# Right-side SBUF tiles moved down by 992 bytes, to whole KBs

## The chip, the cores and the metric

The kernel runs on one core of a Trainium2 chip. The metric is the time of the device for one execution, in microseconds (us), as the median over several runs. Three runs of the kernel before gave 1609.98, 1612.35 and 1612.64 us.

## What is computed

Two layers of a diffusion transformer on 512 latent tokens and 256 context tokens with 1024 features, all in float32. Cut to what matters:

```
for i in range(2):
    mod = split(silu(c) @ ada_w[i] + ada_b[i], 6)          # one set for latents, one for context
    h   = rmsnorm(x, norm_mix_g[i]) * (1 + mod[1]) + mod[0]
    x  += mod[2] * (recurrence(h) if i == 0 else latent_attention(h))
    h   = rmsnorm(x, norm_ffn_g[i]) * (1 + mod[4]) + mod[3]
    g, u = split(h @ ffn_w_in[i], 2)                       # 1024 -> 2 x 2816
    x  += mod[5] * ((silu(g) * u) @ ffn_w_out[i])          # 2816 -> 1024
return rmsnorm(x_latent, final_norm_g)
```

In layer 0 context tokens are carried along everywhere. In layer 1 they only feed keys and values, so the feed-forward part of layer 1 has 512 tokens.

## The kernel before

Features lie on the 128 partitions, tokens along the free dimension: the latents are columns 0 to 511 of a row of 768, the context columns 512 to 767. Every large product is made in three passes. A weight tile and an activation tile are each kept as two float32r parts (h for high, l for low) whose sum is the float32 value, and `mm3` (line 671) issues wh x xh, wh x xl and wl x xh for each feature tile. The weights (128x128) are loaded into TensorE, the activations move through it, and each matmul has a weight load of its own.

The activations that move are of two kinds. The normed and modulated activations, hh and hl, are written by `norm_tile` (line 553: VectorE makes nt, ScalarE hh, VectorE hl) and read by the input products of the recurrence (p, g, u), of the attention latents (ckv, kr, cq) and of the feed-forward part (f, f00g and so on). All others are made inside a stage: ah and al (the gated hidden features, read by the products fo), uh and ul (read by the gates ga), mh and ml (read by lo), cqh and cql (read by q), oh and ol (read by wo), kh and kl (read by the scores s).

In layer 0 most products go over both groups of tokens, so a 512-column matmul and a 256-column matmul alternate (48 matmuls a product with 8 feature tiles). In layer 1 the input products of the feed-forward part and cq take the 512 latent tokens alone. So do two entry phases, in `entry` (line 611), where the products of the second group of tokens follow its norm.

Weights come through `Stream` (line 62): the SP queue loads them whole, ScalarE copies the high part (line 103), VectorE or GpSimd makes the low part (line 115). The modulation vectors come from ada_w: tiles "ada" of 128x1024 are loaded by GpSimd's queue (line 212). In layer 0 they move through TensorE (line 480), in layer 1 VectorE sums them up (lines 430 to 440).

The order of the work on each engine is written out by hand (the strings START, ATTENTION and STEPS); from `manual_schedule` (line 172) on nothing reorders it. Two stacks share each partition's memory. Pools from the left grow up, and pools with side="right" grow down from the end at 229344 bytes, which is 223 KB and 992 bytes. The right side holds, in turn:

```
tile             from line   begins at (bytes)   over a whole KB   bytes
hh0              154         180192              992               24576
hl0              155         204768              992               24576
ada (2 buffers)  211         172000, 176096      992               4096 each
wh, wl of "more" 1335        221152, 225248      992               4096 each
hh1, hl1         1345        188384, 204768      992               16384 each
```

Every tile on the left that a product of line 675 reads begins at a whole KB: ah at 103 KB, al at 127 KB, cqh at 119 KB, kh at 177 KB (and 180 KB), the weights wh and wl from 37 KB to 69 KB. A feature tile's row is 3072 bytes in hh0, hl0, ah and al, and 2048 in hh1 and hl1. The weights of the first unit of layer 1's feed-forward part come from "more"; all other weights lie on the left.

Of the kernel before, what the change touches and what calls it, by code (L numbers as in the profile page):

```python
# [9 lines left out]
F32 = mybir.dt.float32  # L10
# [25 lines left out]
ENTRY_AT = (12, 6)   # products of the first group that follow the statistics, and the spread  # L36
# The first norm and its first products in the order of their parts, see the layer
# [5 lines left out]
# Latent attention in the order of its parts: a letter and its arguments, see mla_mix  # L43
# [18 lines left out]
class Stream:  # L62
    """Weights in the order in which TensorE takes them: loaded whole, split into two float32r
    parts whose sum is the float32 value."""
# [45 lines left out]
    def _low(self, i):  # L110
        """Second part of a unit: what the first leaves of the float32 value."""
        load, n, pieces = self.units[i]
        raw, (hi, lo) = self.raw[load], self.tiles[i]
        for dst, src in pieces:
            self.low_engine.tensor_tensor(dst(lo), src(raw), dst(hi).bitcast(F32), op=ALU.subtract)  # L115
        self.loads[load][2] -= 1
        if self.loads[load][2] == 0:
            del self.raw[load]
            self.fill()
# [20 lines left out]
def kernel(ctx, tc, x, c, ctx_in, c_ctx, ada_w, ada_b, norm_mix_g, norm_ffn_g, ffn_w_in,  # L140
# [11 lines left out]
    hstack, adastack = ExitStack(), ExitStack()  # L152
    hpool = hstack.enter_context(tc.tile_pool(name="h0", bufs=1, side="right"))
# [34 lines left out]
    # shift and scale of the first norm, in parts of the features: first tile, tiles  # L188
# [47 lines left out]
    def std_units(w, col0, ncols, row0=0, kt=KT, ucols=P):  # L236
        """Columns [col0, col0 + ncols) of w as one load, in units of ucols columns."""
        ln = st.load(kt * ncols, lambda t: nc.sync.dma_start(
            t[:, :kt * ncols].rearrange("p (k n) -> p k n", k=kt),
            w[row0:row0 + kt * P, col0:col0 + ncols].rearrange("(k p) n -> p k n", p=P)))  # L240
        ids = []
        for u in range(ncols // ucols):
            dst = lambda t: t[:, :kt * ucols].rearrange("p (k n) -> p k n", k=kt)
            src = lambda t, u=u: t[:, :kt * ncols].rearrange("p (k n) -> p k n", k=kt)[
                :, :, u * ucols:(u + 1) * ucols]
            ids.append(st.unit(ln, kt * ucols, [(dst, src)]))
        return ids
# [14 lines left out]
    # The recurrence in the order of its parts. n = block of 256 features, k = feature tile in it, d = direction:  # L262
    # u n k = input tile, c n k = its convolution, g n k = gate branch tile, G n k = its gelu,
    # t T n d k = gates, w = next weights, e n d k = decay and gated input, q n d k = scale of the input, s n d k = states,
    # m n = gated states of a block, o n m = tile of the output product, a = part of a modulation vector
# [105 lines left out]
    gcol = lambda w: cols_b[:, 96 + w * 8:96 + w * 8 + 8]  # mix0 mix1 ffn0 ffn1  # L371
# [6 lines left out]
    def ada0_step(q, kq):  # L378
        """Products of a part of the first two chunks: groups of columns j = (chunk, tile)."""
        if kq == 0:  # L380
            ada_ps["q"] = psa.tile([P, 512], F32, name=f"psada0{q}", tag="ada")
        ps = ada_ps["q"]
        t = ada0_tiles.pop((q, kq))
        w = PARTS0[q][1]
        for k2 in range(QK):
            k = kq * QK + k2
            for j in range(2 * w):
                c0 = j % w * P
                pe.matmul(ps[32 * j:32 * j + 32, :P], csil[:, k, :], t[:, k2, j // w, c0:c0 + P],
                          start=k == 0, stop=k == KT - 1)  # L390
# [15 lines left out]
    def ada_evac(wait=False):  # L406
        """Columns of a finished chunk; a step after its products, so that TensorE does not wait."""
        if ada_state["evac"] is None:
            return
        i, l, ch, sb = ada_state["evac"]  # L410
        if wait and ada_state["calls"] < 2:
            ada_state["calls"] += 1
            return
        ada_state["evac"] = None
        px = ps_aux(f"adax{i}")
        for cc in range(2):
            pe.transpose(px[:, cc * P:(cc + 1) * P], sb[:, cc * P:(cc + 1) * P], ident)
        pv = px[:, :256].rearrange("p (c j r) -> p j c r", c=2, j=4)
        for v in range(2):
            dve.tensor_tensor(mod[:, l, ch, v, :].rearrange("p (j c) -> p j c", j=4), pv[:, :, :, v],  # L420
                              adab(l, ch).rearrange("p (j c) -> p j c", j=4), op=ALU.add)
        if ch in (1, 4):
            w = l + (2 if ch == 4 else 0)
            for v in range(2):
                dve.scalar_tensor_tensor(gm[:, w, v, :], mod[:, l, ch, v, :], 1.0, gcol(w),
                                         op0=ALU.add, op1=ALU.mult)

    def ada_sum(i, t, ch, k):
        """One feature tile of a chunk of layer 1 on VectorE; a later product with ones adds up the partitions."""
# [95 lines left out]
    def rstd(ss, dst, n):  # L525
        """dst = (ss / n + eps) ** -0.5, tokens on partitions."""
        dve.tensor_scalar(dst, ss, 1.0 / n, EPS, op0=ALU.mult, op1=ALU.add)
        act.activation(dst, dst, AF.Sqrt)
        dve.reciprocal(dst, dst)

    def col_rstd(sqs, s, n, name):
        """rst of the tokens of s, from the partial sums of squares in the tiles sqs."""
# [8 lines left out]
    def diagonals(s, name):  # L541
        """rst of the tokens of s on diagonals; bcast spreads them."""
        dg = tmp.tile([P, T], F32, name=f"dg_{name}", tag="nt")
        for i, t in enumerate(tiles_of(s)):
            dve.tensor_scalar(dg[:, i * P:(i + 1) * P], ident, rst[:, t:t + 1], None, op0=ALU.mult)
        return dg

    def bcast(s, dg, R):
        """R[p, token] = rst of the tokens of s, on all partitions."""
# [3 lines left out]
    def norm_tile(k, w, l, ch, R, roff, group, hh, hl):  # L553
        """Modulated norm of feature tile k, tokens of the group, into hh; returns what makes hl."""
# [10 lines left out]
    class Norm:  # L565
        """Norm and modulation of one group of tokens, in pieces that stand between other work."""
# [23 lines left out]
    def boundary(last_group, na, after=lambda i: None, at=(1, 3, 2)):  # L590
        """The last products of a stage for the second group of tokens, and the norm of the first."""
# [19 lines left out]
    def entry(units, na, nb, nk=2, at=ENTRY_AT):  # L611
        """First products of a stage: the first group of tokens while the norm of the second is made.
        units: (unit, PSUM tile, offset, with the first group)."""
# [39 lines left out]
    def residual(m, ps, l, ch, group, stat):  # L653
        """x tile m += gate * product; the sum of squares on the way where a norm comes next."""
# [16 lines left out]
    def mm3(ps, wh, wl, xh, xl, parts, first, last, off=0):  # L671
        """ps += w^T x in three passes of the split parts."""
# [18 lines left out]
    Rs = acc  # L691

    # recurrence constants
# [10 lines left out]
    def lru_constants():  # L704
        """softplus(-lambda) by its series of atanh, in three pieces; the gates' biases."""
# [27 lines left out]
    # The norm of the first layer and the products that take its tiles as they come  # L733
# [56 lines left out]
    def lru_out(n, m, mt, group, stat=False):  # L790
        """Two feature tiles of the state times w_out, tile m of the result."""
# [12 lines left out]
    def gate(n, d, kk, g, uh, ul):  # L804
        """Gate product g of direction d, feature tile kk of block n."""
# [13 lines left out]
    def decay(n, d, kk, y):  # L819
        """Decay a, the square of the input's scale and the gated input."""  # L820
# [15 lines left out]
    def states(n, d, kk):  # L836
        """Input term and the state sequence."""
# [193 lines left out]
    def mla_mix():  # L1031
# [42 lines left out]
        def rope(dst, src, sh, scale):  # L1074
            """dst = scale * rotated src."""
# [18 lines left out]
        # latents: statistics, norms, the rotated key  # L1094
# [58 lines left out]
        # keys, values and queries of the heads: products (small letters) and their float32r parts  # L1153
# [33 lines left out]
        def uses(u, n):  # L1187
            """The n-th use of a unit is its last."""
# [20 lines left out]
        # rotated queries of two heads: their float32r parts on the two halves of the partitions, so that  # L1209
        # one pass of 128 rows carries two of the three products  # L1210
# [21 lines left out]
        # scores and softmax of 128 queries, transposes, products with the values for 256  # L1232
# [120 lines left out]
    class Final:  # L1353
        """Last norm of one group of tokens, back to tokens on partitions."""
# [23 lines left out]
        def last(self):  # L1378
            """The same with the last feature tile's squares apart, on both engines, in halves."""
# [29 lines left out]
def _rope_tables():  # L1409
    """cos and signed sin of the two axial positions, features on rows, tokens on columns."""  # L1410
# [32 lines left out]
```

## Time and profile before

| | us |
|---|---|
| runs, median of 3 | 1612.35 |
| runs, lowest and highest | 1609.98, 1612.64 |
| profiled execution, span from first to last instruction | 1610.0 |
| profiled execution, its own time | 1610.0 (the page gives the span; the lowest run is 1609.98) |
| TensorE busy in the span | 1556.2 |
| VectorE, ScalarE, GpSimd busy | 807.4, 603.7, 254.1 |

A matmul's listed duration overlaps with that of the next one: matmuls are pipelined. What a matmul costs in a steady stream is therefore the step from its start to the next start, which the chain of waits gives as time over count. [...]

### The profile page before, as it was taken

What the parts mean: (1) busy time and instruction counts of PE and PEld (TensorE: products, weight loads), DVE (VectorE), ACT (ScalarE), POOL (GpSimd) and SP (SyncE); (2) the same over time, 40 slices, a digit from 0 to 9 for tenths busy, and PEclk for the clock granted to TensorE, in tenths of its full rate; (3) what the DMA queues carried; (4) which work ended last, traced back from release to release, by engine and by line L of the source; (5) the groups of instructions that cost most, each with busy time, mean ns of one, the idle gap of its engine ahead of it and who ended that gap; (6) DMA issues with size and microseconds to landing.
All of it is one profiled execution on the core that took longest, in us unless ns stands there. A gap on an engine that the chain in (4) does not pass through costs nothing.

```text
span 1610.0 us, 20936 instructions
## 1 busy us (share of the span) xinstructions
PE 1556.2 (97%) x8895; PEld 1320.6 (82%) x8895; DVE 807.4 (50%) x1068; ACT 603.7 (37%) x812; POOL 254.1 (16%) x212
## 2 busy tenths in 40 slices
PE   7999988979999999999999999999998999999998
PEld 5887877868888888888888877888888888888887
DVE  5666768686545433443322466655536343233234
ACT  5486564733221111221122233666644232232223
POOL 3233332350000000000000323111125000000002
PEclk8999999999999999999999999999999999999999
DMA  9333343220344333344311222110011223223222
GB/s 358 117 108 129 105 131 105 97 87 26 107 137 139 116 121 114 115 141 138 103 55 40 66 60 69 29 42 27 27 66 66 79 89 121 79 82 127 79 66 92
DMA packets 121406, 155.09 MB, mean 96 GB/s; under 512 B 5212, under 2 KB 104145, under 8 KB 121313
## 3 DMA queue, kind: packets, MB, share of 16 engines
q1 hardware_dynamic: 109456, 112.21, 21.2%
q0 software_dynamic: 11552, 41.02, 7.8%
q8 instruction: 70, 1.15, 0.3%
q10 hardware_dynamic: 304, 0.53, 0.1%
q14 instruction: 24, 0.19, 0.0%
HBM read 151.64 MB, written 2.10 MB: 95 GB/s over the span
## 4 chain that ended last, share of the span: by engine, by line
PE 84%; DVE 11%; ACT 3%; issue 1%; DMA 0%; SPq 0%; DVEq 0%; ACTq 0%
PE fo L675 18%; PE f L675 14%; PE s L1242 4%; PE lo L675 3%; PE ga L675 3%; PE wo L675 2%; PE o L1284 2%; PE p L675 2%; PE g L675 2%; PE t L1260 1%; DVE yc L782 1%; DVE tg L845 1%; DVE hl L561 1%; PE u L675 1%; PE q L675 1%
## 5 line engine op out<-in xcount | busy, mean ns | idle before, releaser
L103 ACT ACTIVATE wh<-raw 128x1024 fp32r<-128x1024 f32 (+2 forms) x195 | 191.3, 1011 | 195.1 <-PE fo L675 154.9
L115 POOL TENSOR_TENSOR wl<-raw,wh 128x1024 fp32r<-128x1024 f32 (+3 forms) x66 | 155.5, 2367 | 337.9 <-ACT wh L103 296.6
L675 PE MATMUL fo<-ah,wl 128*128 128x512 f32 (+1 forms) x552 | 167.5, 348 | 0.0
L675 PE MATMUL fo<-ah,wh 128*128 128x512 f32 (+1 forms) x552 | 167.5, 348 | 0.0
L675 PE MATMUL fo<-al,wh 128*128 128x512 f32 (+1 forms) x552 | 167.0, 347 | 0.0
L115 DVE TENSOR_TENSOR wl<-raw,wh 128x1024 fp32r<-128x1024 f32 (+1 forms) x129 | 151.1, 1199 | 2.7 <-ACT wh L103 2.6
L675 PE MATMUL f<-hl,wh 128*128 128x512 f32 x336 | 130.7, 393 | 0.0
L675 PE MATMUL f<-hh,wl 128*128 128x512 f32 x336 | 130.7, 393 | 0.0
L675 PE MATMUL f<-hh,wh 128*128 128x512 f32 x336 | 130.7, 393 | 0.0
L669 POOL TENSOR_TENSOR acc<-acc,sq 128x256 f32<-128x256 f32 (+1 forms) x52 | 51.6, 994 | 494.9 <-ACT sq L667 487.6
L656 DVE SCALAR_TENSOR_TENSOR xT<-fo,mod,xT 128x512 f32<-128x512 f32 (+1 forms) x76 | 46.6, 636 | 155.5 <-PE fo L675 155.2
L212 POOL DMA_DIRECT2D ada<-in_ada_w_dram x78 | 41.9, 538 | 511.5 <-DVE ada L440 384.6
L995 ACT ACTIVATE ah<-sg 128x768 fp32r<-128x768 f32 (+1 forms) x44 | 32.5, 739 | 196.0 <-DVE sg L994 196.0
L675 PEld LDWEIGHTS fo<-ah,wh 128*128 128x128 f32 x552 | 93.5, 189 | 14.7 <-ACT wh L103 0.4
L675 PEld LDWEIGHTS fo<-ah,wl 128*128 128x128 f32 x552 | 93.4, 189 | 13.6
L675 PEld LDWEIGHTS fo<-al,wh 128*128 128x128 f32 x552 | 93.2, 188 | 13.5
L994 DVE TENSOR_TENSOR sg<-sg,f 128x512 f32<-128x512 f32 (+1 forms) x21 | 14.7, 700 | 144.1 <-ACT sg L993 141.1
L675 PEld LDWEIGHTS f<-hh,wh 128*128 128x128 f32 x336 | 62.6, 188 | 15.0
L675 PEld LDWEIGHTS f<-hh,wl 128*128 128x128 f32 x336 | 62.6, 188 | 14.9
L675 PEld LDWEIGHTS f<-hl,wh 128*128 128x128 f32 x336 | 62.6, 188 | 14.9
L993 ACT ACTIVATE sg<-f 128x512 f32<-128x512 f32 x20 | 12.0, 598 | 155.0 <-PE f L675 155.0
L440 DVE SCALAR_TENSOR_TENSOR ada<-ada,csil,ada 128x1024 f32<-128x1024 f32 x42 | 53.9, 1282 | 32.1 <-DMA ada<-in_ada_w_dram 31.6
(656 smaller groups left out, 3480.9 us busy)
## 6 DMA issues: line engine op xcount, KB each, us to landing
raw<-in_ffn_w_in_dram SPq DMA_DIRECT2D x44, 1024.0 KB, 4.9
ada<-in_ada_w_dram POOLq DMA_DIRECT2D x78, 512.0 KB, 4.1
raw<-in_ffn_w_out_dram SPq DMA_DIRECT2D x16, 1024.0 KB, 4.9
ada<-in_ada_w_dram SPq DMA_DIRECT2D x32, 256.0 KB, 5.5
raw<-in_ffn_w_out_dram SPq DMA_DIRECT2D x8, 768.0 KB, 4.6
raw<-in_lru_w_in_dram SPq DMA_DIRECT2D x10, 512.0 KB, 5.0
raw<-in_lru_gate_w_dram SPq DMA_DIRECT2D x16, 256.0 KB, 3.0
raw<-in_lru_w_out_dram SPq DMA_DIRECT2D x8, 512.0 KB, 4.0
```

What stands on the lines that cost most here:

```text
L103: nc.scalar.activation(dst(hi), src(raw), AF.Copy)
L115: self.low_engine.tensor_tensor(dst(lo), src(raw), dst(hi).bitcast(F32), op=ALU.subtract)
L212: eng.dma_start(t, ada_w[l, k * P:(k + 1) * P, ch * D:(ch + 1) * D])
L440: dve.scalar_tensor_tensor(t, t, csil[:, k, 0:1], ada_ps["lat"], op0=ALU.mult, op1=ALU.add)
L561: return lambda: dve.scalar_tensor_tensor(hl[:, k, s], t[:, :n], mod[:, l, ch, v, k:k + 1], hh[:, k, s].bitcast(F32), op0=ALU.add, op1=ALU ...
L656: dve.scalar_tensor_tensor(xT[:, m, s], ps[:, s], mod[:, l, ch, v, m:m + 1], xT[:, m, s], op0=ALU.mult, op1=ALU.add)
L669: accs.append(lambda: nc.gpsimd.tensor_tensor(acc[:, s], acc[:, s], sq[:, s], op=ALU.add))
L675: pe.matmul(ps[:, off + s.start:off + s.stop], a, b[:, s], start=first and i == 0, stop=last and i == 2)
L782: dve.scalar_tensor_tensor(y[:, s0:s1], ps[:, s0 + o:s1 + o], convw(tap, k), y[:, s0:s1], op0=ALU.mult, op1=ALU.add)
L995: act.activation(ah[:, j, :n], sg[:, :n], AF.Copy)
L1242: pe.matmul(ps[:, o:o + 384], x, y[:, k0:k1], start=j == 0, stop=j == 4)
L1284: pe.matmul(ps[:, :256], x[:, t % 4, hs], y[:, t, :], start=t == 0 and j == 0, stop=t == NT - 1 and j == 2)
```

## The change

A pool "skip" is opened on the right side before all others, with one tile of 248 float32 values in each partition (992 bytes), which GpSimd fills with zeros once and which nothing reads. All later tiles of the right side thus begin 992 bytes lower: hh0 at 179200 bytes (175 KB), hl0 at 203776 (199 KB), hh1 at 187392 (183 KB), hl1 at 203776 (199 KB), the ada tiles at 171008 and 175104 (167 and 171 KB), the weights of "more" at 220160 and 224256 (215 and 219 KB). The left side stays where it is. The rest of the diff takes out comments and doc strings.

```diff
     tmp = ctx.enter_context(tc.tile_pool(name="tmp", bufs=2))
     hstack, adastack = ExitStack(), ExitStack()
+
+    skip = ctx.enter_context(tc.tile_pool(name="skip", bufs=1, side="right")).tile([P, 248], F32, name="skip")
+    nc.gpsimd.memset(skip, 0.0)
     hpool = hstack.enter_context(tc.tile_pool(name="h0", bufs=1, side="right"))
     hh = hpool.tile([P, KT, T], F32R, name="hh0")
     hl = hpool.tile([P, KT, T], F32R, name="hl0")
```

## Rows read from the trace of the kernel before

**Rows 1.** The page: span, busy time of each engine, and the chain's shares by engine.
```profile
span 1610.0 us, 20936 instructions
...
PE 1556.2 (97%) x8895; PEld 1320.6 (82%) x8895; DVE 807.4 (50%) x1068; ACT 603.7 (37%) x812; POOL 254.1 (16%) x212
...
PE 84%; DVE 11%; ACT 3%; issue 1%; DMA 0%; SPq 0%; DVEq 0%; ACTq 0%
```

**Rows 2.** Windows, layer 1: PE, PEld, DVE, ACT, POOL busy us (count), clock, DMA share, GB/s.
```profile
1254.00:1321.00 67.00, 67.00 (x289) 53.94 (x288) 22.18 (x24) 18.78 (x24) 0.00 (x0) 1.00 0.29 95
1321.00:1365.00 44.00, 44.00 (x196) 36.40 (x195) 16.98 (x19) 11.79 (x13) 0.00 (x0) 1.00 0.35 114
```

**Rows 3.** Chain of waits, 512-column streams of layer 1: start, us, engine, product, line, matmuls.
```profile
967.19 4.90 PE cq L675 x21
...
1188.10 5.50 PE wo L675 x24
...
1248.57 5.60 PE f11g L675 x24
1254.17 67.20 PE f L675 x288
1321.37 43.55 PE fo L675 x192
1364.91 89.60 PE f L675 x384
1454.51 43.55 PE fo L675 x192
1498.06 67.20 PE f L675 x288
```

**Rows 4.** Chain of waits inside the entry phases of layer 0 and layer 1.
```profile
380.58 0.70 PE f01g L675 x3
```
```profile
956.70 1.40 PE ckv L675 x6
```

**Rows 5.** Chain of waits, layer 0, products with 512 and 256 columns in turn.
```profile
411.74 8.48 PE f002u L675 x48
...
506.44 25.44 PE fo L675 x144
...
618.24 8.32 PE f012u L675 x48
...
711.76 24.98 PE fo L675 x144
```

**Rows 6.** Timeline of TensorE, scores of layer 1 (384 columns, two a row).
```profile
1048.99 0.51 PE L1242 MATMUL s<-kl,qh 128*128 128x384 f32 x2
1049.34 0.51 PE L1242 MATMUL s<-kh,ql 128*128 128x384 f32 x2
```

**Rows 7.** Timeline of TensorE, modulation products: 128 columns from the left, 256 from ada.
```profile
24.94 1.52 PE L389 MATMUL psada<-ada,csil 128*32 128x128 f32 x48
```
```profile
108.10 1.07 PE L480 MATMUL psada<-ada,csil 128*32 128x256 f32 x16
```

**Rows 8.** Groups by line and form: line, engine, operation, shapes, count | busy us, mean ns.
```profile
L561 DVE SCALAR_TENSOR_TENSOR hl<-nt,mod,hh 128x512 fp32r<-128x512 f32 x24 | 18.0, 749 | 3.6 <-ACT hh L560 3.0
L782 DVE SCALAR_TENSOR_TENSOR yc<-u,cols_d,yc 128x511 f32<-128x511 f32 x12 | 9.0, 746 | 3.7 <-ACT yc L778 3.4
...
L558 DVE SCALAR_TENSOR_TENSOR nt<-xT,gm,R_m1b 128x512 f32<-128x512 f32 x8 | 5.9, 748 | 4.1 <-PE R_m1b L551 3.9
```

**Rows 9.** Timeline of all engines at the start.
```profile
0.74 0.20 POOL masks.py:197 MEMSET ident<- 128x128 f32 x1 [0.29 <-POOLq L1429]
...
2.08 0.31 POOL masks.py:199 TENSOR_SCALAR_AFFINE_SELECT ident<-ident 128x128 f32<-128x128 f32 x1
...
4.55 7.03 PE L506 MATMUL xtr<-ident,xtok 128*128 128x128 f32 x40 [1.10 <-DMA xtok<-in_ctx_dram]
...
22.18 0.48 PE L513 MATMUL pt<-ident,rows_b 128*128 128x128 f32 x1
```

## The prediction, written before the run

> **What bounds the kernel now.** I read the page first: TensorE is busy for 97% of the 1610.0 us span and the chain of work that ended last is 84% TensorE [rows 1]. An edit that leaves every instruction where it is can gain only if it shortens a step of that chain. [...]
>
> Then I read the chain as steps, time over count. The products f, f11g and cq, which move hh and hl, take 67.20 / 288 = 89.60 / 384 = 5.60 / 24 = 4.90 / 21 = 233.3 ns a matmul. The products fo, which move ah and al, take 43.55 / 192 = 226.8 ns [rows 3]. Both have 512 columns, fresh weights for each matmul, the same clock, and no gap. [...] The difference, **6.5 ns a matmul**, is the whole matter.
>
> What separates the kinds? Not the pitch of a row: cq moves hh0 (3072 bytes a row) and f moves hh1 (2048), and both step at 233.3, while ah has 3072. [...]
>
> **The change, part by part.**
>
> *Streams of 512 columns on hh and hl.* In layer 1's feed-forward part they are 24 + 288 + 384 + 288 = 984 matmuls, all in the chain [rows 3]. Cq adds 3 tiles x 8 x 3 = 72, the latent group of ckv and kr another 72, and the latent group of layer 0's entry 72. In the entry phases the step is the same, 0.70 us for three and 1.40 for six [rows 4]; per feature tile the nine matmuls take 2.1 us against 2 x 0.75 = 1.5 us of VectorE making the next tile (nt 748 ns, hl 749 [rows 8]), so TensorE leads there too and goes on leading at 9 x 226.8 = 2.04. Together 1200 matmuls x 6.5 ns = 7.8 us. The quick step is not reached at once: wo, 24 matmuls on oh at whole KBs behind a stop, takes 5.50 us [rows 3], 0.06 over 24 x 226.8 ns. I take off 0.3 us, an estimate of five such restarts, since the chain shows the f streams without a stop. Sum **-7.5 us**. From below: if the cause is not the address, 0. From above: 7.8.
>
> *Alternating 512 and 256 columns, layer 0.* Here hh and ah do not differ in kind. Products of 48 matmuls on hh come at two paces, 8.32 us (173.3 ns a matmul) and 8.48 (176.7). Products on ah and al show the same two: 24.98 / 144 = 173.5 and 25.44 / 144 = 176.7 [rows 5]. The chain lists 15 products on hh at 8.32 or 8.33 and 24 at 8.46 to 8.48, and three more at 8.52 look like quick ones with a stop in them. The quick ones stand together in the chain, seven from f012g on and eight from f022g on, so a product mostly keeps the pace of the one before it. The pace is a state of the stream that both addresses allow, and it is drawn anew when times shift. I take 0, with ends: of about 57 such products (44 of the feed-forward part, 13 of the recurrence) 18 are quick; all quick gives 39 x 0.16 = 6.2 us, all slow costs 18 x 0.16 = 2.9 us. A likely draw is within 2.5 us either way.
>
> *Modulation loads.* In layer 0 four groups of 256-column products from the ada tiles take 1.07 us; twelve of 128 columns from tiles on the left, at whole KBs, take 1.52 us [rows 7]. Per group that is 0.268 against 2 x 0.127 = 0.253, so at most 0.015 x 64 groups = 0.9 us could come, and I take 0: the first matmul after a stop is in either. In layer 1 VectorE sums them up, off the chain.
>
> *The norms' writes.* VectorE's hl at 512 columns takes 749 ns, yc on the left with the same operation 746 [rows 8]. The address costs VectorE nothing that is seen. For ScalarE's write of hh I have no twin; it waits for VectorE's nt in all these phases, so 0.
>
> *Extra weights of "more".* One unit, read in an entry as the stationary side: 0.
>
> *The fill of the skip tile.* It adds one GpSimd memset ahead of the identity matrix. 128x128 took 0.20 us, so 248 columns are about 0.20 x 248 / 128 = 0.39 us. The identity is ready at 2.39 us, and the transposes that begin the chain's work wait for their data until 4.55 [rows 9]. The delay lies under that: 0. Without that cover it would be 0.4 us. GpSimd's queue of small loads is moved back by the same 0.4 us, and what they bring is first used at 22.18 us.
>
> Sum: 1610.0 - 7.5 = 1602.5 us for the profiled execution. Its own time stands 2.4 us below the median of the runs shown, near the lowest (1609.98), so I take the sum from the median: 1612.35 - 7.5 = 1604.85, given as **1604.8 us**. The before's own spread, 2.7 us, is of the size of layer 0's draw.
>
> [...]
>
> **The rivals.**
>
> *The address does nothing.* The two paces of layer 0 speak for it: there aligned and unaligned tiles behave alike, so the 233.3 of layer 1 could be a state too, one that f and cq happen to fall into and fo not. Against it: f holds 233.3 in three separate stretches and cq in its own, fo returns to 226.8 in both, and no stretch of either kind shows the other's step [rows 3]. Time: 1612.35, give or take 1.5. This is also the case in which the change does not do what it says.
>
> *Layer 0 gains as well.* If streams at whole KBs settle in the quick pace more often, up to 6.2 us come on top: 1604.85 - 6.2 = 1598.7. Against it: ah, at whole KBs, shows the slow pace in layer 0 as well [rows 5].
>
> *Both reads in step: slower.* TensorE reads weights and moving tiles at once. With hh at whole KBs as the weights are, the two could meet more often, and the streams on hh settle in the slow pace throughout layer 0 while layer 1 keeps its 233.3. Price: +2.9 us, 1610.0 + 2.9 = 1612.9 on the profiled execution's base and 1615.2 on the median's. It decides only where layer 1 gains less than 2.9 us, that is under 450 of the 1200 matmuls. Against it: fo on ah, at whole KBs with the same weights, is the quicker kind [rows 3].
>
> *Half of it.* Only hh1's streams gain, or each 512-column stream falls in either state: -3 to -4 us, about 1608.8.
>
> **How the numbers follow.** Chances: the forecast 0.70, the address does nothing 0.13, layer 0 gains as well 0.06, half of it 0.07, slower 0.04. Below 0.2% of 1612 us, or 3.2 us, a measurement cannot tell this kernel from no change, given its spread of 2.7 us. The forecast, the gain in layer 0 and a good part of "half" are faster by more: 0.70 + 0.06 + 0.04 = 0.80. The rest of "half" and most of "does nothing" are within: 0.15. Slower: 0.05. The forecast's own range is 1602 to 1607.5, by the draw of layer 0. The range for 8 in 10 reaches down into "layer 0 gains as well", to 1600.0, and up to 1611.0, which takes in "half" and the lower edge of "does nothing".
>
> **What would show it.** Right: in the chain of the changed kernel f x288 takes about 65.3 us and f x384 about 87.1 (226.8 a matmul), cq x21 about 4.76, the entries' threes 0.68, while fo x192 stays at 43.55 and layer 0's products still come at 8.32 and 8.48. The identity is ready some 0.4 us later and the first transposes start as before. Wrong: f x288 still at 67.2; or f quick and the span not shorter, which would mean that layer 0's products turned to 8.48, or that a wait stands in layer 1 where there is none now.

## The result

The changed kernel took 1598.12 us (median of four runs, 1596.36 to 1599.43) against 1611.68 us for the kernel before (also the median of four): ratio 0.9919, 95% interval 0.9907 to 0.9932, **13.6 us faster**. The forecast was 1604.8, with 1600.0 to 1611.0 as its range; the time lies 1.9 us below the range. Its direction and its main term came out, and more came on top of them.

The changed kernel's profiled execution took 1599.43 us with a span of 1597.7, so 1.7 us lie around the span. The profiled execution before, whose own time was given as its span, thus took about 1611.7. The forecast was made from the median, so nothing changes in it.

The page of the changed kernel, the lines that answer to [rows 1]:

```profile
span 1597.7 us, 20937 instructions
...
PE 1545.6 (97%) x8895; PEld 1319.3 (83%) x8895; DVE 806.0 (50%) x1068; ACT 603.8 (38%) x812; POOL 256.2 (16%) x213
...
PE 84%; DVE 11%; ACT 3%; issue 1%; DMA 0%; SPq 0%; DVEq 0%; ACTq 0%
```

The span is 12.3 us shorter and TensorE is busy 10.6 us less. The one more instruction is the fill. The other 1.7 us of the span are time in which TensorE stood idle before.

The chain of waits of the changed kernel: layer 1's 512-column streams and two of the entries' steps, as in [rows 3, 4]. All line numbers are 3 higher.

```profile
381.96 0.68 PE f01g L678 x3
...
953.81 1.36 PE ckv L678 x6
...
959.93 4.76 PE cq L678 x21
...
1242.86 5.47 PE f11g L678 x24
1248.33 65.28 PE f L678 x288
1313.61 43.52 PE fo L678 x192
1357.13 87.04 PE f L678 x384
1444.17 43.52 PE fo L678 x192
1487.69 65.28 PE f L678 x288
```

65.28 / 288 = 87.04 / 384 = 226.7 ns: f now steps as fo does (43.52 / 192 = 226.7), f11g comes near it (5.47 / 24 = 227.9), and fo has stayed where it was.

Where the rest came from is seen stage by stage. These are windows cut at the first matmul of each stage: recurrence, layer 0's entry, the rest of layer 0's feed-forward part, latents and attention, layer 1's feed-forward part (wo, 62.5 us in both, is left out). First the kernel before, then the changed one (columns as in [rows 2]).

```profile
62.30:361.40 299.10, 277.23 (x1659) 227.26 (x1656) 209.32 (x234) 180.93 (x204) 106.21 (x74) 0.96 0.35 113
361.40:402.90 41.50, 39.68 (x210) 34.48 (x209) 25.62 (x40) 14.67 (x21) 4.29 (x3) 0.92 0.08 26
402.90:933.30 530.40, 529.76 (x3065) 459.47 (x3064) 221.48 (x244) 108.72 (x135) 42.94 (x61) 1.00 0.33 107
933.30:1162.90 229.60, 221.83 (x1307) 190.75 (x1305) 137.57 (x210) 130.49 (x207) 40.15 (x22) 0.98 0.12 36
...
1225.40:1594.90 369.50, 365.45 (x1706) 302.07 (x1705) 140.23 (x175) 102.84 (x138) 16.89 (x14) 1.00 0.26 87
```

```profile
61.80:356.80 295.00, 275.72 (x1658) 225.94 (x1655) 207.60 (x234) 180.96 (x204) 107.92 (x74) 0.97 0.36 115
356.80:397.70 40.90, 39.12 (x209) 34.48 (x208) 25.56 (x40) 14.67 (x21) 4.32 (x3) 0.92 0.08 26
397.70:926.60 528.90, 528.03 (x3064) 459.32 (x3063) 221.69 (x244) 108.78 (x135) 43.04 (x61) 1.00 0.34 108
926.60:1155.50 228.90, 220.98 (x1307) 190.63 (x1305) 137.59 (x210) 130.49 (x207) 40.14 (x22) 0.98 0.12 36
...
1218.00:1582.60 364.60, 360.52 (x1707) 303.69 (x1706) 140.22 (x175) 102.85 (x138) 16.92 (x14) 1.00 0.27 88
```

Layer 1's feed-forward part gains 4.9 us, the recurrence 4.1, layer 0's feed-forward part 0.6 + 1.5, the latents 0.7, the start 0.5. The start can't be put down to the change: the recurrence begins at 62.3 us in the kernel before and at 61.2 in the first run below, whose tiles begin 992 bytes over as well. The prediction had no term for the recurrence. In the recurrence only 1.5 of the 4.1 us is less busy time (277.23 to 275.72, at a granted TensorE clock of 0.97 of full speed after 0.96); 2.6 is less idle time. The list of TensorE's waits has one entry that changed by as much. Before:

```profile
PE ga L675 <- DVE yc L782: 5.1, 1, 5.1
```

and after:

```profile
PE ga L678 <- DVE yc L785: 2.3, 1, 2.3
```

The timeline around it, first before, then after, shows why: VectorE's sum at line 847 (850) takes 3.60 us in the one and 0.96 in the other. Its columns are start, us, engine, line, operation.

```profile
268.52 0.57 POOL L212 DMA_DIRECT2D ada<-in_ada_w_dram  x1 [5.10 <-PE psada L480]
268.72 3.60 DVE L847 TENSOR_TENSOR tg<-tg,tg 128x768 f32<-128x768 f32 x1
269.11 2.39 POOL L115 TENSOR_TENSOR wl<-raw,wh 128x1024 fp32r<-128x1024 f32 x1
```

```profile
266.82 0.57 POOL L215 DMA_DIRECT2D ada<-in_ada_w_dram  x1 [5.18 <-PE psada L483]
266.94 0.96 DVE L850 TENSOR_TENSOR tg<-tg,tg 128x768 f32<-128x768 f32 x1
267.41 2.73 POOL L115 TENSOR_TENSOR wl<-raw,wh 128x1024 fp32r<-128x1024 f32 x1
```

Before, VectorE's sum is not done until 272.32, which is 0.82 us after GpSimd's subtraction ends (269.11 + 2.39 = 271.50). After, it is done at 267.90, and GpSimd's subtraction, 2.73 us long instead of 2.39, ends 2.24 us after that. VectorE makes the gates' input yc right behind this sum, and TensorE's ga waits for yc; no wait of TensorE in the recurrence is put down to GpSimd's wl, before or after. There are eight such sums. In the kernel before, three others take 2.97 to 2.99 us, and in the changed kernel one that had taken 0.96 takes 2.97; apart from the wait for yc, no entry in the list of TensorE's waits there grew by more than 0.4 us.

### The profile page after: what moved, and what is told of

Read it like the earlier page. It is cut to its first block, busy times and chain, and to the rows that moved or that the text cites. A ratio compares the mean times of both kernels' runs of the same rounds, so it can differ in the third digit from the quotient of the medians.

```text
span 1597.7 us, 20937 instructions
## 1 busy us (share of the span) xinstructions
PE 1545.6 (97%) x8895; PEld 1319.3 (83%) x8895; DVE 806.0 (50%) x1068; ACT 603.8 (38%) x812; POOL 256.2 (16%) x213
## 4 chain that ended last, share of the span: by engine, by line
PE 84%; DVE 11%; ACT 3%; issue 1%; DMA 0%; SPq 0%; DVEq 0%; ACTq 0%
PE fo L678 18%; PE f L678 14%; PE s L1245 4%; PE lo L678 3%; PE ga L678 2%; PE wo L678 2%; PE o L1287 2%; PE p L678 2%; PE g L678 2%; PE t L1263 1%; DVE yc L785 1%; DVE hl L564 1%; DVE tg L848 1%; PE u L678 1%; PE k L678 1%
## 5 line engine op out<-in xcount | busy, mean ns | idle before, releaser
L678 PEld LDWEIGHTS f<-hl,wh 128*128 128x128 f32 x336 | 62.5, 188 | 12.9
L678 PEld LDWEIGHTS f<-hh,wl 128*128 128x128 f32 x336 | 62.5, 188 | 12.8
```

Of the source, the lines that this page charges most:

```text
L678: pe.matmul(ps[:, off + s.start:off + s.stop], a, b[:, s], start=first and i == 0, stop=last and i == 2)
```

## The experiments

Three questions: is it the begin of the tiles, and which begins are quick; which part of the change brings how much; and what made the recurrence shorter. Each quoted text names its own theories. Three of them in the later texts: that the 0.7 us by which all work shifts in time changed the clock in the recurrence (A), that the ada tiles' begin did (B), that VectorE's sum and GpSimd's subtraction changed places (C). Diffs are against the changed kernel unless said otherwise.

**Other begins.** The skipped tile gets another length, all else stays. With 256 values (1024 bytes) all right-side tiles move by a whole KB and begin 992 bytes over one again.

```diff
-    skip = ...tile([P, 248], F32, name="skip")
+    skip = ...tile([P, 256], F32, name="skip")
```

> The skip tile has 256 columns instead of 248, so the right-side tiles move by 1024 bytes and begin 992 bytes past a whole KB again; the memset and the pool stay. If only the begin within a KB counts: f x288 at 67.2 us in the chain, cq x21 at 4.90, and the time of before, 1611 us. If the move itself, the memset or the added pool counts: some or all of the 13.6 us stay, 1598 to 1606.

1610.07 us against 1611.62, ratio 0.9994 (0.9984 to 1.0004): no change. F x288 is at 67.20 again and cq at 4.90. So neither the fill nor the move brings anything; what counts is where within a KB a tile begins.

With 8 values the tiles begin at 960 over a whole KB, with 16 at 928:

```diff
-    skip = ...tile([P, 248], F32, name="skip")
+    skip = ...tile([P, 8], F32, name="skip")
```

> The skip tile has 8 columns (32 bytes), so the right-side tiles begin 960 bytes past a whole KB: a multiple of 64 and not of 128. If a grain of 64 bytes or less counts: f x288 at 65.3 us and the time of after, 1598. If whole KBs (or 128 bytes or more) are needed: f x288 at 67.2 and 1611.

1614.5 us, ratio 1.0018 (1.0008 to 1.0027): slower by 2.9 us, where the text had the time of before or of after. The chain of waits:

```profile
409.53 8.46 PE f002u L678 x48
...
616.32 8.48 PE f012u L678 x48
...
1254.58 67.20 PE f L678 x288
```

```diff
-    skip = ...tile([P, 248], F32, name="skip")
+    skip = ...tile([P, 16], F32, name="skip")
```

> The skip tile has 16 columns (64 bytes), so the right-side tiles begin 928 bytes past a whole KB: a multiple of 32 and not of 64, as before. If the grain is 64 bytes: f x288 at 67.2 us, 1611. If it is 32 bytes or less, before would have been fast already, so that is excluded; if any small move helps: 65.3 and 1598.

1605.81 us, ratio 0.9971 (0.9960 to 0.9982), which is neither case of the text: f stays slow, and yet 4.7 us are gained. Its chain:

```profile
408.66 8.32 PE f002u L678 x48
...
613.28 8.32 PE f012u L678 x48
...
1247.85 67.47 PE f L678 x288
```

Both begins leave the 512-column step slow (233.3 and 234.3 ns). The alternating products of layer 0 differ: on hh0 at 960 all are slow (8.46 us or more for the 48), at 928 all are quick (8.32 to 8.34, and four of 8.52 that look like quick ones with a stop in them). So for these begins the pace of layer 0 is set by the begin; what holds at 0 and 992, where both paces occur, is seen further down.

**Layer 1 alone.** The tile is opened ahead of layer 1's tiles: hh1, hl1 and "more" at whole KBs, hh0, hl0 and ada at 992.

```diff
-    skip = ctx.enter_context(...)          # ahead of hh0
...
+        skip = ctx.enter_context(tc.tile_pool(name="skip", bufs=1, side="right")).tile([P, 248], F32, name="skip")
```

> The skip tile is made only ahead of the pool more, so hh1, hl1 and the extra weights begin at whole KBs and hh0, hl0 and the ada tiles stay as before. By the forecast's term for layer 1: 984 matmuls x 6.5 ns, f x288 at 65.3, f x384 at 87.1, -6.4 us, 1605. If the rest of the gain (6 us, mostly between 200 and 290 us) comes from layer 0's tiles it is missing here; if it were chance of the runs, a part of it may appear: 1599 to 1605.

1604.17 us, ratio 0.9961 (0.9947 to 0.9974), that is 6.3 us less. F x288 takes 65.28 us and cq still 4.90.

**hh0 and hl0 alone, and ada alone.** First a tile that goes with hh0's pool and another that puts the ada tiles back to 992; then one ahead of the ada tiles alone.

```diff
-    skip = ctx.enter_context(...)
+    skip = hstack.enter_context(...)
...
+    skip2 = adastack.enter_context(tc.tile_pool(name="skip2", bufs=1, side="right")).tile([P, 8], F32, name="skip2")
```

> Only hh0 and hl0 begin at whole KBs; the ada tiles (by a second skip of 32 bytes), hh1, hl1 and the extra weights stay 992 bytes past one. Theory A (the recurrence's 5 us come from TensorE's clock, which fell for a shorter time because the work before ran some 0.7 us earlier): hh0's products bring the work forward, so the -5 us at 290 us are here, and cq, ckv and layer 0's entry give 0.9: 1604 to 1606. Theory B (the ada tiles' address makes VectorE or TensorE faster in the recurrence): -5 us missing, 1609 to 1611.

1606.67 us (ten runs, 1603.1 to 1610.1), ratio 0.9982 (0.9972 to 0.9991), between the two ranges of the text. Its chain has cq quick and f slow, as it should:

```profile
958.72 4.76 PE cq L680 x21
...
1245.56 67.20 PE f L680 x288
```

VectorE's sum takes 0.96 us here, and the recurrence 294.5 us in its profile; layer 0's feed-forward part takes 530.5, as in the kernel before. Its runs scatter by 7 us, more than any other kernel's here, and the profiled one, at 1603.12, is the fastest of the ten, 3.6 us below their median. Whether the sum got ahead in the others too is not shown.

```diff
-    skip = ctx.enter_context(...)          # ahead of hh0
+    skip = adastack.enter_context(...)     # behind hl0, ahead of ada
```

> Only the ada tiles begin at whole KBs; hh0, hl0, hh1, hl1 and the extra weights stay. Theory A: nothing comes forward before 200 us, 1611, the clock's low stretches at 214 and 275 us of 6.8 us each as before. Theory B: about -5 us in the recurrence, 1606.

1610.36 us, ratio 0.9999 (0.9990 to 1.0009): nothing. The ada tiles' begin alone does not shorten the recurrence (298.4 us, the sum 3.60). Of the two stretches at the lower granted clock (0.50 in the kernel before) that the text named, the one at 275 us came with its 6.8 us, the one at 214 took 3.4. By the ratios the parts bring 6.3 + 2.9 + 0.2 = 9.4 us together, 3.6 to 4.2 less than the whole.

**The left side moved off.** A tile of 32 bytes below all left-side activation tiles; the weights and the right side stay at whole KBs.

```diff
+    off = ctx.enter_context(tc.tile_pool(name="off", bufs=1)).tile([P, 8], F32, name="off")
+    nc.gpsimd.memset(off, 0.0)
```

> After, with 32 bytes put in ahead of the pool big on the left: xT, ah, al, uh, cqh, oh, kvh and so on begin 32 bytes past a whole KB, the weights and the right side stay at whole KBs. If the address of the moving tile is the cause, the penalty goes over to the left streams: fo x192 from 43.5 to 44.8 us, f x288 stays at 65.3; 524 fo matmuls and some 230 of lo, q, qr and wo at 512 columns x 6.5 ns = 4.9 us, 1603. If it is a matter of the right side: fo x192 stays at 43.5, 1598.

1602.44 us, ratio 0.9950 (0.9935 to 0.9965). By the ratios that is 5.0 us more than the changed kernel (1610.27 x 0.0031), near the 4.9 of the text, but in part for another reason: VectorE's sum is the late one here (3.60 us), and the recurrence takes 298.0 us where the changed kernel took 295.0. The chain:

```profile
503.26 24.96 PE fo L680 x144
...
1248.66 65.28 PE f L680 x288
1313.94 44.80 PE fo L680 x192
```

Now fo has the slow step in layer 1 (233.3) and f the quick one. The side of the memory and the kind of tile are out as causes of the step: the begin decides. In layer 0 the same tile, 32 over, is quick (24.96 / 144 = 173.3 ns).

**The shift in time alone.** Seven transposes that nothing reads, at about 62 us, give back what the start and the first norm gained.

```diff
+    dly = ps_aux("dly")
+    for _ in range(7):
+        pe.transpose(dly[:, :P], ident, ident)
```

> After, with seven more 128-column transposes of the identity on TensorE at about 62 us, 0.76 us in all, which nothing reads. Theory A (the place of the work against TensorE's clock): the low stretches at 214 and 275 us are 6.8 us long again and the recurrence ends some 5 us later: 1603. Theory B (addresses): only the 0.8 us of the transposes: 1599.

1598.84 us, ratio 0.9930 (0.9915 to 0.9945). VectorE's sum still takes 0.96 us, the recurrence 293.9, and by the ratios the delay costs 1.8 us with an interval that holds the 0.8 that the text reckons for the transposes. The profile doesn't show the delay that was meant, though: its recurrence starts at 61.22 us, ahead of the changed kernel's 61.76, since the start was quicker in this execution. What speaks against theory A is the comparison with the run with 256 values: there the recurrence starts at 61.19 us, the same moment, and the sum takes 3.60 us and the recurrence 298.9. So the moment at which the work comes does not decide it.

**VectorE's sum earlier in the kernel before.** Half of one multiply ahead of the sum is left out (384 of 768 columns), so the sum comes 0.4 us earlier against GpSimd's work.

```diff
+        c = 384 if (n, d, kk) == (2, 1, 1) else T
-        dve.tensor_tensor(b, b, ti, op=ALU.mult)
+        dve.tensor_tensor(b[:, :c], b[:, :c], ti[:, :c], op=ALU.mult)
```

> Before, no tile moved; in one step of the recurrence (block 2, reverse direction, second tile) VectorE multiplies 384 of 768 columns, half the product left out, so that the sum behind it (at 268.7 us in before, 3.60 us long) starts some 0.4 us earlier. Theory C (that sum and GpSimd's weight subtraction at 269.1 us keep each other out, and who comes first decides): the sum takes 0.96 us, the wait of the gates behind it shrinks by 2.6 us and a shorter low stretch of TensorE's clock adds about 1: -3 to -4.5 us, 1606 to 1608. Theory B (the tiles' addresses): -0.4 us, 1610.

1606.53 us against 1610.06, ratio 0.9982 (0.9973 to 0.9992): 2.9 us less by the ratio, 3.5 by the medians. The sum got ahead; the second view is the window of the recurrence:

```profile
267.37 0.96 DVE L849 TENSOR_TENSOR tg<-tg,tg 128x768 f32<-128x768 f32 x1
267.55 0.57 POOL L213 DMA_DIRECT2D ada<-in_ada_w_dram  x1 [5.09 <-PE psada L481]
268.14 2.43 POOL L115 TENSOR_TENSOR wl<-raw,wh 128x1024 fp32r<-128x1024 f32 x1
```

```profile
61.10:356.00 294.90, 275.72 (x1659) 225.46 (x1655) 207.86 (x234) 180.99 (x204) 106.09 (x74) 0.97 0.36 115
```

0.4 us less work on VectorE bring 2.9 to 3.5: theory C's price, in the kernel before and without any tile moved. In the profile the recurrence takes 294.9 us instead of 299.1, with the busy time that it has in the changed kernel (275.72), and all later stages take what they took before (41.5, 530.4, 229.6, 62.5 and 369.5).

**VectorE's sum later in the changed kernel.** Two fills of the skipped tile by VectorE ahead of the sum.

```diff
+            if (n, d, kk) == (2, 1, 1):
+                for _ in range(2):
+                    dve.memset(skip, 0.0)
```

> After, with two fills of the skip tile by VectorE, some 0.27 us each, ahead of the same sum, which nothing reads. Theory C: the sum falls behind GpSimd's subtraction again and takes about 3.6 us instead of 0.96; +3 to +4.5 us, 1601.5 to 1603. Theory B: +0.5 us, 1598.6.

1597.88 us, ratio 0.9926 (0.9911 to 0.9941), and not the 1601.5 to 1603 of theory C. In the trace the edit did what it should: GpSimd's subtraction starts first and the sum takes 3.14 us.

```profile
265.71 0.57 POOL L215 DMA_DIRECT2D ada<-in_ada_w_dram  x1 [5.18 <-PE psada L483]
266.30 2.38 POOL L115 TENSOR_TENSOR wl<-raw,wh 128x1024 fp32r<-128x1024 f32 x1
266.37 3.14 DVE L853 TENSOR_TENSOR tg<-tg,tg 128x768 f32<-128x768 f32 x1
```

TensorE's wait for yc is 5.1 us and the recurrence 297.5, 2.5 more than in the changed kernel. By the ratios the total is only 1.1 us above the changed kernel's (1610.06 x 0.0007), which the intervals don't tell from nothing. The profiles say more. Against the changed kernel's first profile the loss seems to be made up later, but there layer 0's entry, the latents and layer 1's feed-forward part were longer (40.9, 228.9 and 364.6 us, here 39.6, 227.9 and 363.0), the entry at a granted clock of 0.92 where it is 0.96 here. The changed kernel's second profile, further down, has these stages as here (39.5, 228.1 and 363.0), and against it this one is longer by 2.4 us in span (1595.7 and 1593.3), by the recurrence's 2.5. So the loss is where C puts it and nothing made it up; the medians of four runs do not resolve it.

**Two grids.** Layer 0's alternating products on begins that gave only the quick pace (right 928, left 32), layer 1 at whole KBs.

```diff
-    skip = ctx.enter_context(...).tile([P, 248], F32, name="skip")
+    skip = hstack.enter_context(...).tile([P, 16], F32, name="skip")
...
+    off = lru.enter_context(tc.tile_pool(name="off", bufs=1)).tile([P, 8], F32, name="off")
+    nc.gpsimd.memset(off, 0.0)
...
+            if l == 0:
+                off0 = es.enter_context(...).tile([P, 8], F32, name="off0")
+                nc.gpsimd.memset(off0, 0.0)
...
+        skip1 = ctx.enter_context(...).tile([P, 248], F32, name="skip1")
+        nc.gpsimd.memset(skip1, 0.0)
```

> All activation tiles of layer 0 that move through TensorE begin off the whole KB (hh0, hl0 and ada 928 bytes past one; uh, ul, mh, ml, ah, al 32 bytes past one), all of layer 1 at whole KBs (hh1, hl1 and the extra weights by a skip of 992 bytes made only there). If the address sets the pace of either kind of stream: layer 0's products all at 8.32 us, 1320 pairs on hh0 save 3 to 4 ns each and 770 on the left 2 to 4 against after, some 6 us, and 216 streams of 512 columns on hh0 lose 6.5 to 7.5 ns, 1.5 us: -4.5 us against after, 1592 to 1596, with up to 4 us on top where VectorE's sum in the recurrence loses against GpSimd. If the quick pace of 64 bytes and of the left at 32 was chance: 1598 to 1602.

1593.28 us (1592.68 to 1595.42), ratio 0.9897 (0.9883 to 0.9912): the fastest of all medians, though its interval touches the changed kernel's. Of the products of 48 matmuls that its chain lists 39 come at 8.32 or 8.33 and none at 8.46 to 8.49, the slow pace; in the changed kernel these are 22 and 18. Lines of the chain:

```profile
608.79 8.32 PE f012u L678 x48
...
701.52 24.96 PE fo L678 x144
...
1241.58 65.28 PE f L678 x288
```

Layer 0's feed-forward part takes 525.1 us instead of 528.9. Cq is back at 4.92, and the sum lost to GpSimd (3.41 us), so some more may be left to gain; no run tried it.

**The changed kernel once more**, with nothing edited.

> The changed kernel as it is, profiled a second time; nothing is edited. Theory C (part of the gain is the recurrence's: VectorE's sum at about 267 us gets ahead of GpSimd's weight subtraction, and does so by when they start): if the outcome belongs to the kernel, the sum takes 0.96 us again, TensorE's wait for yc 2.0 to 2.3 us, the recurrence about 295 us, and the median is 1597 to 1600. Rival D (the outcome is drawn anew in each execution, within the 0.5 us in which starts scatter): the sum takes 3.1 to 3.6 us, the wait 5.1, the recurrence 297 to 298.5, and the profiled execution is 1600 to 1603 or the loss is made up elsewhere as it was with two fills ahead of the sum. In either case f x288 takes 65.28 us and f x384 87.04, since that term belongs to the address.

1595.52 us (1594.52 to 1599.13) against 1609.29, ratio 0.9920 (0.9900 to 0.9939): the ratio of the first time, though the median lies below the 1597 to 1600 of the text. VectorE's sum is ahead again:

```profile
266.36 0.57 POOL L215 DMA_DIRECT2D ada<-in_ada_w_dram  x1 [5.19 <-PE psada L483]
266.47 0.96 DVE L850 TENSOR_TENSOR tg<-tg,tg 128x768 f32<-128x768 f32 x1
266.95 2.72 POOL L115 TENSOR_TENSOR wl<-raw,wh 128x1024 fp32r<-128x1024 f32 x1
```

The recurrence is 295.0 us again, so the outcome was the same in both executions of this kernel that were profiled. What differs between the two is layer 0's entry (39.5 against 40.9), the latents (228.1 against 228.9) and layer 1's feed-forward part, whose window answers to the last one above:

```profile
1215.20:1578.20 363.00, 358.94 (x1706) 302.03 (x1705) 140.19 (x175) 102.82 (x138) 16.85 (x14) 1.00 0.27 88
```

363.0 is 6.5 below the 369.5 of before; the first profile's 364.6 held a stretch of 3.4 us at a granted clock of 0.5 at 1228 us, in the entry, that this one doesn't have.

## Why the prediction fell short

**Streams of 512 columns: right.** Forecast 7.5 us. F and cq fell to the steps that were named (65.3, 87.1, 4.76), and so did the entries' threes (0.68). Over all 1200 steps on hh and hl, counted in the traces from each such matmul's start to the next start, the mean went from 233.9 to 227.3 ns: 1200 x 6.6 = 7.9 us. Layer 1's part of that is seen whole in the second profile (6.5 us); in the first a stretch at the lower clock hides some of it (4.9). That the begin is the cause was the author's estimate; the other begins show that it is, and nothing else of the change: on hh the step is 226.7 ns at 0 and 233.3 to 234.3 at 928, 960 and 992, on ah 226.7 at 0 and 233.3 at 32. "The address does nothing" is refuted.

**Modulation loads, the norms' writes, "more", the fill: right at 0.** The fill took 0.30 us from 0.74 on, and the identity's select ended at 2.43 instead of 2.39 [rows 9], 0.04 us later and not 0.4; the transposes started at 4.54. ScalarE's hh and VectorE's hl at 512 columns took 724 and 749 ns before and after.

**Alternating products, "I take 0": off by 1.5 us, inside its ends, for a reason that does not hold.** The chain lists 22 products of 48 matmuls at 8.32 or 8.33 instead of 15. Even on ah and al, whose begin did not move, the pair of 512 and 256 columns took 348.8 ns instead of 351.0 (mean over the feed-forward part). The prediction took the pace for a state that both begins allow and that is "drawn anew when times shift". At 928, 960 and 32 one pace is all there is (8.32 us, 8.46 to 8.48, and 24.96 for the 144 of fo). At 0 and 992 both occur, but which product gets which is not drawn. From layer 0's f on, the chain lists 41 products of 48 matmuls, and their times agree one by one, within 0.01 us, between the kernel before and the runs with 256 values, with layer 1 alone, with ada alone and with the halved multiply, the last of which comes 5.4 us earlier. In another order they agree as closely between the changed kernel, its second profile, the transposes and the fills. First two lines of the changed kernel, then the same two in the run with the fills:

```profile
406.61 8.33 PE f002u L678 x48
...
611.22 8.48 PE f012u L678 x48
```

```profile
407.17 8.33 PE f002u L678 x48
...
611.78 8.48 PE f012u L678 x48
```

In the kernel before these two are 8.48 and 8.32 [rows 5]. With hh0 and hl0 alone at whole KBs there is a third order, and layer 0's feed-forward part gains nothing (530.5 us); nor does it with the ada tiles alone (530.6). With the left side in its place, and begins of 0 and 992 alone, the 1.5 us came only where both hh0 and ada begin at whole KBs (528.7 to 528.9 in four profiles). So the places of the tiles fix the order, and moves of the time up to 5.4 us don't change it; how they fix it no run shows.

**The step that failed** is the sum itself, which took the recurrence over as it was. "An edit that leaves every instruction where it is can gain only if it shortens a step of that chain" holds, but the parts priced only TensorE's own steps there. The recurrence is where TensorE waits for VectorE, and VectorE's sum lay across GpSimd's subtraction, 2.64 us longer than the same sum just ahead of it (3.60 and 0.96). The trace of before showed that: a wait of 5.1 us in one piece. A reader of the waits would have had a term of up to 2.8 us that hangs on which engine comes first, to be put into the range. The stage gave 4.1 us. Of these the order of the two was worth between 2.5 (the fills, 297.5 after 295.0) and 4.2 (the halved multiply, 294.9 after 299.1, its own 0.4 included), a shorter stretch at the lower clock among them: over the stretch from 266 to 290 us the granted clock is 0.86 in all nine profiles in which the sum is late, and TensorE's wait for yc is 5.0 or 5.1 us; in the five in which it is not late, the wait is 2.0 to 2.3 and the clock 0.93 or 1.00. With the stage's 4.1 the sum is 1612.35 - 7.5 - 4.1 - 1.5 = 1599.25, within the spread of the changed kernel's runs.

When the order changes: in all fourteen profiles the outcome goes by how far VectorE's sum starts behind GpSimd's issue of the ada load just ahead of its subtraction. At 0.12 us or less (this kernel twice, 0.12 and 0.11; hh0 alone 0.11; the transposes 0.11; the halved multiply, 0.18 us ahead of it) it takes 0.96 us; at 0.15 or more (before, 0.20; 960, 0.15; the fills, 0.66; all others) 3.1 to 3.6. All four profiles with hh0 at whole KBs, the left side unmoved and nothing put ahead of the sum have it early, with hh0 and hl0 alone among them, so their begin was enough. The change moved the two against each other by 0.08 us. GpSimd's issue waits for TensorE's products psada, so a quicker stream on hh0 could do that; this last step is argued and not shown.

In all nine profiles in which the sum is late it ends 0.82 or 0.83 us after GpSimd's subtraction, the kernel before and the two grids among them. Which came first is not to be read off the listed starts: in the kernel before, VectorE's is 0.39 us ahead (268.72 and 269.11), with the fills 0.07 us behind (266.37 and 266.30), and it takes 3.60 us in the one and 3.14 in the other. Why the sum takes longer beside the subtraction no run shows.

**The rivals.** "Layer 0 gains as well", at 1598.7, named nearly the time, but that was luck: the pace brought 1.5 us and not 6.2, and the recurrence, which it does not name, brought the rest. "Both reads in step: slower" did not come. Matmuls and weight loads do run side by side (busy for 360.52 and 303.69 of the 364.60 us of layer 1's feed-forward part in the changed kernel), and its picture exists: the begin at 960 puts every alternating product on hh0 at the slow pace and costs 0.18%.

**What stays open.** Why the begin sets the step is not settled: 960 is a multiple of 64, 928 of 32, and both are as slow as 992 (233.3, 234.3 and 233.3 ns). Nor is the grain known: 0 is the only quick begin of the five, and 64, 128, 256 or 512 over a whole KB were not tried. And the weights of all these 512-column streams begin at whole KBs, so whether the moving tile's begin counts by itself or against that of its weights is open. Nor is it settled what makes the stretches at the lower clock come shorter in some executions; the two profiles of the changed kernel differ by 4.4 us in span (1597.7 and 1593.3), mostly by them. And the whole brought about 4 us more than its parts one by one. Two things bear on that, and neither was run by itself: layer 0's 1.5 us need hh0 and the ada tiles together, and the median of hh0 alone stands 3.6 us above the one execution in which its sum was seen to be early.

## What to carry to other kernels

Compare the step of streams that should be equal, and if one is slower, look at the begin of its tile within a KB: 992 bytes a partition were worth 0.8% here, the recurrence's part included. Then read the waits of the stages that TensorE doesn't fill, because a shift of 0.08 us between VectorE and GpSimd went with a sum of 0.96 us instead of 3.60 here, and that was worth a third to a half of the streams' gain. Put such a contest into the range, or take it out of the kernel by moving the work of the engine that has time.

## What the runs showed that was not expected

The begin sets two things that don't go together (ns; the step is time over count of f x288 or fo x192 in the chain, the pair a mean over the trace, from one 512-column start to the next, without steps over 400 ns):

| begin over a whole KB | 512-column step | 512 + 256 pair, layer 0's feed-forward part |
|---|---|---|
| 0 (hh, changed kernel) | 226.7 | 349.7, both paces |
| 992 (hh, before) | 233.3 | 350.4, both paces |
| 960 (hh) | 233.3 | 353.2, slow only |
| 928 (hh) | 234.3 | 346.7, quick only |
| 32 (ah, al) | 233.3 | 346.8, quick only |

The begin that is best for a stream of 512 columns is thus not the best for 512 and 256 in turn, and a kernel with both can gain from a begin of its own for each, as the two grids did in layer 0 (525.1 us after 528.9).
